# Attention scores as float32 products of 64 rows at two row positions of the array

## The chip, the cores and the metric

The kernel runs on one core of a Trainium2 chip. The metric is the time of one execution on the device in microseconds, of which the median of several runs is taken. The profile shows one execution: PE is TensorE's product, PEld its weight load (which can run behind a product), DVE is VectorE, ACT is ScalarE, POOL is GpSimd, SP is SyncE, which here issues DMAs.

## The reference

One layer of a decoder trunk on x of 512 tokens by 1024 channels (batch 1, one layer). An input projection of the normalised and modulated x gives queries, keys and values for two attentions and two gates.

```
qa, ka, va, qd, kd, vd, ga, gd = split(h @ w_in)
# sliding window: 8 query heads of 64, 2 key/value heads (4 query heads share one),
# blocks of 128 queries against the block before and their own, ALiBi, a sink per head
scores = einsum('bnqkgd,bnskd->bnkgqs', qb, kb) * 64 ** -0.5       # then mask, bias, softmax with sink, times values
# differential: 4 heads with 2 maps of 64 each, blocks of 128 queries against all keys, causal, ALiBi
scores = einsum('bqhmd,bshmd->bhmqs', qblk, k) * 64 ** -0.5
a = softmax(scores)[:, :, 0] - lam * softmax(scores)[:, :, 1]      # then times values, RMSNorm per head
merged = sigmoid(ga) * (out_a @ w_branch_swa) + sigmoid(gd) * (out_d @ w_branch_diff)
x = x + gate1 * (merged @ w_out)                                   # then a gated convolutional MLP and a last norm
```

Every score is a sum over only 64 channels. All arrays are float32.

## The kernel before

Weights and activations that go through TensorE are split into a high and a low part in the format float32r: the high part is a rounded copy (ACT), the low part is source minus high (DVE). A product of two split operands is then three TensorE instructions (`mm3`, L123 to L125: high by high, high by low, low by high). Tokens lie along the free axis: a projection unit (`steps`) multiplies eight blocks of a weight tile into one PSUM bank of 128 output channels by 512 tokens.

The stages in order of time: opening sums and modulation; the first projections over eight blocks k (`product`, into eight accumulators `acc`); the attentions with the rest of the projections; the merge; the output projection; the MLP (`up`, then `dc`).

In the attention stage TensorE's order is written out by hand (`manual_schedule`). `fill(n)` issues n steps of whatever projection unit is next (queries `pqa`, differential queries `pq` and keys `pk`, gates `pga`, branches `pA`); between the fills stand the attention's own products. The constants `SWA_FILL` and `DIFF_FILL` say how many steps lie between. ACT and DVE take their work in an order that a planner makes from priorities, `issue_after` and, at the opening of the stage, a second hand-written order.

Sliding window: four pairs i, each of the heads i and i + 4, which use the two key heads. `swa_scores(i, n0)` makes the scores of two query blocks n0 and n0 + 1 for both heads j (L581), 128 keys wide for block 0 and 256 for the others, into one bank per head (`sbank`, three in rotation). DVE adds the bias and takes the maximum (L587), ACT takes the exponential (L602), DVE normalises (L610); `swa_transpose` (L621) turns the result, and `swa_values` (L632) multiplies by the values as float32 products, the two heads at two column positions (columns 0 to 63 and 64 to 127).

Differential: 16 steps s, head h = s // 4 and query block n = s % 4, with n + 1 blocks of keys. `diff_scores` (L679) makes both maps m, 128 to 512 columns wide. Steps 0 and 1 of a head go as one group, steps 2 and 3 each alone, so there are 12 groups; the sliding window has eight.

A score's operands fill 128 rows although it sums over 64 channels. For one head, `stack` writes the query's high part (ACT) into the 64 rows that the head owns and its low part (DVE) into the other 64. `double` writes the key's high part, then its low part, into both halves of rows. Two float32r products with the same stacked query, first by the high key and then by the low key, give all four cross terms:

```
for b in range(2):
    nc.tensor.matmul(sps[j][:, n - n0, :w], qa[:, i, j, qs], ka[:, j, b, ks], start=b == 0, stop=b == 1)
```

For the first key tile and the first query tile the copies stand in the opening order by hand (L476 to L490); the low part of query pair 1 is made after the first scores. The key tile `ka` serves all four pairs; each differential head has a tile `qk` of six planes (two query planes, four key planes).

Of the kernel before, what the change touches and what calls it, by code (L numbers as in the profile page):

```python
# [8 lines left out]
F32 = mybir.dt.float32  # L9
F32R = mybir.dt.float32r  # L10
AF = mybir.ActivationFunctionType
ALU = mybir.AluOpType
PSUM = bass.MemoryType.PSUM

P = 128
D = 1024
S = 512
# [30 lines left out]
def kernel(  # L48
# [367 lines left out]

    at = ExitStack()
    ap = pool("att", stack=at)
    qa = big.tile([P, 4, 2, S], F32R, tag="qa", name="qa")
    ka = big.tile([P, 2, 2, S], F32R, tag="kvA", name="ka")  # L420
    lower, upper = slice(0, 64), slice(64, P)
    outa = [big.tile([P, 4, S], F32R, tag=f"out{g}", name=f"outa{g}") for g in "hl"]

# [6 lines left out]
            nc.vector.scalar_tensor_tensor(lo, src, scale, hi.bitcast(F32), ALU.mult, ALU.subtract)  # L430


    halves = ((lower, upper), (upper, lower))

    def stack(dst, src, scale, soon=HP, high=True, low=True):
        with tc.high_priority(offset=soon) if soon else ExitStack():
            sc = [scale if isinstance(scale, float) else scale[own] for own, _ in halves]
            for j in range(2) if high else ():
                own = halves[j][0]
                nc.scalar.activation(dst[own, j], src[own], AF.Copy, scale=sc[j])  # L440
            for j in range(2) if low else ():
                own, other = halves[j]
                nc.vector.scalar_tensor_tensor(
                    dst[other, j], src[own], sc[j], dst[own, j].bitcast(F32), ALU.mult, ALU.subtract
                )

    def double(dst, src, soon):
        with tc.high_priority(offset=soon):
            for j, (own, _) in enumerate(halves):
                nc.scalar.copy(dst[own, j, 0], src[own])  # L450
            for j, (own, _) in enumerate(halves):
                nc.vector.tensor_sub(dst[own, j, 1], src[own], dst[own, j, 0].bitcast(F32))
            for j, (own, other) in enumerate(halves):
                (nc.scalar.copy if j or soon == HP else nc.vector.tensor_copy)(dst[other, j], dst[own, j])

    vv = [big.tile([P, DIFF_HEADS, S], F32R, tag=f"vv{g}", name=f"vv{g}") for g in "hl"]
    vaT = big.tile([P, S], F32, tag="sq2", name="vaT")
# [10 lines left out]
    def load_tile(n, name):  # L468
# [4 lines left out]
    man = ExitStack()  # L473
    man.enter_context(tc.manual_schedule(engines={nc.vector.engine, nc.scalar.engine}))
    first_tiles = [load_tile(TILE_QA + i, f"wqa{i}") for i in (2, 3)]
    nc.scalar.copy(ka[lower, 0, 0], acc[0][lower])  # L476
    nc.scalar.copy(ka[upper, 1, 0], acc[0][upper])
    nc.vector.tensor_sub(ka[lower, 0, 1], acc[0][lower], ka[lower, 0, 0].bitcast(F32))
    nc.vector.tensor_sub(ka[upper, 1, 1], acc[0][upper], ka[upper, 1, 0].bitcast(F32))
    keep_v(3)  # L480
    nc.scalar.activation(qa[lower, 0, 0], acc[1][lower], AF.Copy, scale=qsc[lower, 0:1])
    nc.vector.scalar_tensor_tensor(
        qa[upper, 0, 0], acc[1][lower], qsc[lower, 0:1], qa[lower, 0, 0].bitcast(F32), ALU.mult, ALU.subtract
    )
    nc.scalar.copy(ka[upper, 0, 0], acc[0][lower])
    nc.scalar.copy(ka[upper, 0, 1], ka[lower, 0, 1])
    nc.scalar.activation(qa[upper, 0, 1], acc[1][upper], AF.Copy, scale=qsc[upper, 0:1])
    nc.vector.tensor_copy(ka[lower, 1, 0], acc[0][upper])
    nc.vector.tensor_sub(ka[lower, 1, 1], acc[0][upper], ka[lower, 1, 0].bitcast(F32))
    nc.vector.scalar_tensor_tensor(  # L490
        qa[lower, 0, 1], acc[1][upper], qsc[upper, 0:1], qa[upper, 0, 1].bitcast(F32), ALU.mult, ALU.subtract
    )
    stack(qa[:, 1], acc[2], qsc[:, 1:2], soon=0, low=False)
    keep_v(6, (0,))
    vat_copy = nc.scalar.copy(vaT, acc[5])
    man.close()
# [67 lines left out]
    def swa_scores(i, n0):  # L564
        if n0 == 0:
            c = pairs[i] = Pair()
            c.nm, c.lsum, c.es = (
                ap.tile([P, 2, NT], F32, tag=t, bufs=2, name=f"{t}{i}") for t in ("nm", "lsum", "es")
            )
            c.sb = [ap.tile([P, 2, P], F32, tag="st0", bufs=2, name=f"st{i}_0")]  # L570
            c.sb += [ap.tile([P, 2, 256], F32, tag="st", bufs=ST, name=f"st{i}_{n}") for n in range(1, NT)]
            c.pT, c.copies = [], [None, None]
        c = pairs[i]
        sps = {j: sbank(f"sw{i}_{n0}_{j}", (P, 2, 256)) for j in range(2)}
        order = [(j, n) for j in range(2) for n in (n0, n0 + 1)]
        for j, n in order if i == 0 or n0 else order[::2] + order[1::2]:
            w = P if n == 0 else 2 * P
            k0 = max(0, n - 1) * P
            qs, ks = slice(n * P, (n + 1) * P), slice(k0, k0 + w)
            for b in range(2):  # L580
                nc.tensor.matmul(sps[j][:, n - n0, :w], qa[:, i, j, qs], ka[:, j, b, ks], start=b == 0, stop=b == 1)  # L581
        for j in range(2):
            for n in (n0, n0 + 1):
                w = P if n == 0 else 2 * P
                with tc.high_priority(offset=HP):
                    h = i + 4 * j
                    c.last = nc.vector.tensor_tensor_reduce(  # L587
                        c.sb[n][:, j, :w], sps[j][:, n - n0, :w], dsw[:, 256 - w : 256], -(2.0 ** -(h + 1)),
                        nsink[:, h : h + 1], ALU.add, ALU.min, c.nm[:, j, n : n + 1],
                    )  # L590
# [50 lines left out]
    def add_q(i):  # L641
        def q(wts):
            o = fbank(f"pqa{i}")
            yield from steps(o, wts, hT, KT)
            stack(qa[:, i], o, qsc[:, i : i + 1])

        units.append((None, q))

    def add_head(h):
        def q(wts):  # L650
            t = heads[h] = ap.tile([P, 6, S], F32R, tag="qk", bufs=2, name=f"qk{h}")
            o = fbank(f"pq{h}")
            yield from steps(o, wts, hT, KT)
            stack(t[:, 0:2], o, 2.0 ** (2 * h - 1), HP if h > 1 else HP // 2)

        def k(wts):
            t = heads[h]
            o = fbank(f"pk{h}")
            yield from steps(o, wts, hT, KT)
            double(t[:, 2:6].rearrange("p (j b) s -> p j b s", b=2), o, HP if h > 1 else HP // 2)  # L660

        for run, n in ((q, TILE_QD), (k, TILE_KD)):
            units.append((lambda n=n: load_tile(n + h, f"w{n}_{h}"), run))
# [4 lines left out]
    def diff_scores(*ss):  # L668
        ops = []
        for s in ss:  # L670
            h, n = divmod(s, NT)
            t = heads[h]
            w = (n + 1) * P
            if n == 0:
                firsts[h] = [sbank(f"sd{h}_{m}", (P, 2, 256)) for m in range(2)]
            sps = [firsts[h][m][:, n, :w] if n < 2 else sbank(f"sd{h}_{n}_{m}")[:, :w] for m in range(2)]
            for m in range(2):
                for b in range(2):
                    nc.tensor.matmul(  # L679
                        sps[m], t[:, m, n * P : (n + 1) * P], t[:, 2 + 2 * m + b, :w], start=b == 0, stop=b == 1  # L680
                    )
            ops.append((s, sps, w))
        for s, sps, w in ops:
            h, n = divmod(s, NT)
            mx = ap.tile([P, 2], F32, tag="dmx", bufs=3, name=f"dmx{h}_{n}")
            pm = []
            for m in range(2):
                st = ap.tile([P, w], F32, tag="st", bufs=ST, name=f"sd{h}_{n}_{m}")
                with tc.high_priority(offset=HP):
                    nc.vector.tensor_tensor_reduce(  # L690
                        st, sps[m], ddf[:, 512 - w : 512], -(2.0 ** (-2 * (h + 1))), 3e38, ALU.add, ALU.min,
                        mx[:, m : m + 1],
                    )
                pm.append(st)
            scored[s] = mx, pm
# [149 lines left out]
    with tc.issue_after(pairs[0].last.ins), tc.issue_after(vat_copy.ins):  # L845
        with tc.high_priority(offset=HP):
            keep_v(6, (1,))
            keep_v(4, (1,))
        stack(qa[:, 1], acc[2], qsc[:, 1:2], high=False)
        swa_softmax(0)  # L850
        keep_v(7, (1,))

        lp = cpool.tile([P, 2, 64], F32, tag="part", name="lp")
        ls = cpool.tile([P, 2], F32, name="ls")
        nlam = cpool.tile([P, 1], F32, name="nlam")
        nc.vector.tensor_mul(lp, lamv[:, 0:4:2], lamv[:, 1:4:2])
        nc.vector.reduce_sum(ls, lp, axis=mybir.AxisListType.X)
        nc.scalar.activation(ls, ls, AF.Exp)
        nc.vector.tensor_sub(nlam, ls[:, 1:2], ls[:, 0:1])
        nc.vector.tensor_scalar_add(nlam, nlam, -LAM_INIT)  # L860
        fill(VA_AT)
        turn_va()
        fill(SWA_FILL[2] - VA_AT)
# [1015 lines left out]
```

## Time and profile before

| what | value |
|---|---|
| median of 3 runs | 676.56 us (676.55 to 677.2) |
| span of the profiled execution, first to last instruction | 675.4 us |
| PE busy | 665.2 us (98%), 4021 instructions |
| PEld busy | 591.5 us (88%) |
| DVE busy | 564.1 us (84%) |
| ACT busy | 400.6 us (59%) |
| POOL busy | 85.0 us (13%) |
| mean granted TensorE clock | 0.996 |
| chain that ended last | PE 84%, issue 7%, DVE 4% |

The profiled execution's own time is known only by its span; the median of the runs is 1.2 us longer, which lies around the first and the last instruction. The busy time of PE is the union of its instructions' times; products overlap in the array, their ends are modelled, and so what a product occupies is read from the distance between starts, not from its duration. A row such as "128*128 128x256" gives the loaded operand's rows and columns and then the streamed operand's rows and columns.

### The profile page before, as it was taken

What the parts mean: (1) busy time and instruction counts of PE and PEld (TensorE: products, weight loads), DVE (VectorE), ACT (ScalarE), POOL (GpSimd) and SP (SyncE); (2) the same over time, 40 slices, a digit from 0 to 9 for tenths busy, and PEclk for the clock granted to TensorE, in tenths of its full rate; (3) what the DMA queues carried; (4) which work ended last, traced back from release to release, by engine and by line L of the source; (5) the groups of instructions that cost most, each with busy time, mean ns of one, the idle gap of its engine ahead of it and who ended that gap; (6) DMA issues with size and microseconds to landing.
All of it is one profiled execution on the core that took longest, in us unless ns stands there. A gap on an engine that the chain in (4) does not pass through costs nothing.

```text
span 675.4 us, 10797 instructions
## 1 busy us (share of the span) xinstructions
PE 665.2 (98%) x4021; PEld 591.5 (88%) x4021; DVE 564.1 (84%) x1005; ACT 400.6 (59%) x704; POOL 85.0 (13%) x111
## 2 busy tenths in 40 slices
PE   8999999999999999999999999999999999999995
PEld 7888888888887888888899999999999998888884
DVE  6988997778767678954899998888888899979996
ACT  7678787465745333233696655556655666665664
POOL 2000000002213100010010211011111004441200
PEclk9999999999999999999999999999999999999998
DMA  9961231445255697568365988797886559996803
GB/s 357 417 235 62 94 95 63 132 149 179 89 170 188 236 314 264 189 185 282 92 123 137 227 201 200 203 214 162 187 198 171 132 187 208 198 203 186 157 0 125
DMA packets 72068, 121.78 MB, mean 180 GB/s; under 512 B 4240, under 2 KB 48432, under 8 KB 72016
## 3 DMA queue, kind: packets, MB, share of 16 engines
q1 hardware_dynamic: 53104, 95.04, 41.4%
q0 software_dynamic: 18624, 25.84, 22.8%
q8 instruction: 31, 0.51, 0.3%
q10 hardware_dynamic: 288, 0.21, 0.1%
q14 instruction: 21, 0.17, 0.1%
HBM read 118.97 MB, written 2.11 MB: 179 GB/s over the span
## 4 chain that ended last, share of the span: by engine, by line
PE 84%; issue 7%; DVE 4%; DMA 1%; ACT 1%; POOL 1%; POOLq 0%; ACTq 0%
PE up L1202 33%; PE dc L1808 7%; PE av L371 3%; PE oc L1262 2%; PE oc L1258 2%; PE pgd L124 2%; PE pgd L123 2%; PE oc L1259 2%; PE pgd L125 2%; PE aqa L368 2%; PE pga L123 1%; PE pga L125 1%; PE pga L124 1%; PE sw L581 1%; PE sd L679 1%
## 5 line engine op out<-in xcount | busy, mean ns | idle before, releaser
L1202 PE MATMUL up<-t,m_whi 128*128 128x256 f32 x512 | 93.1, 283 | 0.0
L1202 PEld LDWEIGHTS up<-t,m_whi 128*128 128x128 f32 x512 | 79.9, 192 | 0.0
L1202 PE MATMUL up<-t,m_wlo 128*128 128x256 f32 x256 | 72.4, 283 | 0.0
L1202 PE MATMUL up<-bh,p_whi 128*128 128x256 f32 x232 | 65.7, 283 | 0.0
L1202 PE MATMUL up<-bl,p_whi 128*128 128x256 f32 x232 | 65.7, 283 | 0.0
L1202 PE MATMUL up<-bh,p_wlo 128*128 128x256 f32 x232 | 65.7, 283 | 0.0
L1202 PEld LDWEIGHTS up<-t,m_wlo 128*128 128x128 f32 x256 | 49.2, 192 | 0.0
L1104 POOL DMA_DIRECT2D s<-in_w_up_dram x21 | 27.0, 1367 | 158.5 <-DMA s<-in_w_up_dram 104.8
L1202 PEld LDWEIGHTS up<-bh,p_whi 128*128 128x128 f32 x232 | 44.5, 192 | 0.0
L1202 PEld LDWEIGHTS up<-bl,p_whi 128*128 128x128 f32 x232 | 44.5, 192 | 0.0
L1202 PEld LDWEIGHTS up<-bh,p_wlo 128*128 128x128 f32 x232 | 44.5, 192 | 0.0
L1132 ACT CAST m_whi<-s 128x1024 fp32r<-128x1024 f32 x31 | 32.5, 1048 | 15.7 <-DVE s L1126 9.1
L795 DVE CUSTOM_DVE_ANT_0 ra<-ra,csb 128x1024 f32<-128x1024 f32 x32 | 38.6, 1219 | 3.8 <-DMA ra<-in_w_ada_t_dram 3.7
L1136 DVE TENSOR_TENSOR m_wlo<-s,m_whi 128x1024 fp32r<-128x1024 f32 x31 | 37.7, 1217 | 1.3 <-ACT m_whi L1132 1.3
L1202 PE MATMUL up<-t,p_whi 128*128 128x256 f32 x176 | 32.2, 283 | 0.0
L1202 PEld LDWEIGHTS up<-t,p_whi 128*128 128x128 f32 x176 | 27.4, 192 | 0.1
L705 ACT ACTIVATE sd<-sd,dmx 128x128 f32<-128x128 f32 (+3 forms) x32 | 17.8, 556 | 14.9 <-DVE dmx L690 14.7
L1132 ACT CAST p_whi<-wa 128x1024 fp32r<-128x1024 f32 x18 | 18.8, 1042 | 12.6 <-PE up L1202 9.0
L1209 ACT ACTIVATE gT<-a,cols 128x512 f32<-128x512 f32 x22 | 17.6, 813 | 13.4 <-DVE a L1244 13.0
L1136 DVE TENSOR_TENSOR p_wlo<-wa,p_whi 128x1024 fp32r<-128x1024 f32 x18 | 22.0, 1222 | 4.0 <-ACT p_whi L1132 2.7
L1202 PE MATMUL up<-t,p_wlo 128*128 128x256 f32 x88 | 24.9, 283 | 0.0
L1126 DVE TENSOR_TENSOR s<-s,wa 128x1024 f32<-128x1024 f32 x20 | 24.3, 1217 | 0.1
(551 smaller groups left out, 2036.4 us busy)
## 6 DMA issues: line engine op xcount, KB each, us to landing
ra<-in_w_ada_t_dram SPq DMA_DIRECT2D x32, 512.0 KB, 4.3
wa<-in_w_up_dram SPq DMA_DIRECT2D x22, 512.0 KB, 4.3
s<-in_w_up_dram SPq DMA_DIRECT2D x21, 512.0 KB, 4.7
s<-in_w_up_dram POOLq DMA_DIRECT2D x21, 512.0 KB, 6.8
adaw<-in_w_ada_t_dram SPq DMA_DIRECT2D x15, 512.0 KB, 9.9
a<-in_w_up_dram SPq DMA_DIRECT2D x11, 512.0 KB, 4.8
b<-in_w_down_dram SPq DMA_DIRECT2D x10, 512.0 KB, 4.0
w<-in_w_first_dram SPq DMA_DIRECT2D x8, 512.0 KB, 9.9
```

Of the source, the lines that this page charges most:

```text
L123: nc.tensor.matmul(o, lh, rh, start=start, stop=False)
L124: nc.tensor.matmul(o, lh, rl, start=False, stop=False)
L125: nc.tensor.matmul(o, ll, rh, start=False, stop=stop)
L371: nc.tensor.matmul(acc[i], ht[:, t : t + P], wts[k][w][:, S:], start=start, stop=stop)
L705: nc.scalar.activation(pm[m], pm[m], AF.Exp, bias=mx[:, m : m + 1], scale=-1.0, accum_out=(l0, l1)[m])
L795: nc.vector.tensor_tensor_reduce(r, r, csb, 1.0, 0.0, ALU.mult, ALU.add, late_mod[:, idx : idx + 1])
L1104: nc.gpsimd.dma_start(dst, upblock(*blk), accum_op=ALU.add)
L1126: nc.vector.tensor_add(src, src, R[J, "a11" if name == "m6" else "a12"])
L1132: nc.scalar.copy(W[J, name][0], R[J, SRC[name]])
L1136: nc.vector.tensor_sub(lo, R[J, SRC[name]], hi.bitcast(F32))
L1202: nc.tensor.matmul(o[u], w[:, k, cu], b[:, k], start=name in ("p1", "m5", "p2") and k == 0 and x == 0, stop=k == 3 and x == 2, skip_group_ ...
L1808: nc.tensor.matmul((bank2[u] if o is None else o)[:, sl], a[:, q, cu], b[:, q, sl], start=first_mm and x == 0, stop=last_mm and x == 2, sk ...
```

## The change

Queries and keys are kept as float32, once, in the 64 rows in which the projection leaves them (`keep`, one ACT instruction over all 128 rows, for the first key tile one DVE copy). The head or map j reads rows 0 to 63 or 64 to 127 (`sides[j]`) of both operands, and a score is one float32 product over 64 rows. Products of the two heads, or of the two maps, alternate, at the two row positions of the array, into two banks. `stack`, `double`, the split and the doubling are gone, and so are the hand-written copies of the opening; the tiles shrink (`qa` from eight planes to four, `ka` from four to one, `qk` from six to two). Within a group of the sliding window the order of products becomes block by block, both heads of a block together. The query of pair 1 is kept whole in the opening, where only its high part was.

```
-    qa = big.tile([P, 4, 2, S], F32R, tag="qa", name="qa")
-    ka = big.tile([P, 2, 2, S], F32R, tag="kvA", name="ka")
+    qa = big.tile([P, 4, S], F32, tag="qa", name="qa")
+    ka = big.tile([P, S], F32, tag="kvA", name="ka")
...
-    def stack(dst, src, scale, soon=HP, high=True, low=True):
...
-    def double(dst, src, soon):
...
+    sides = (lower, upper)
+
+    def keep(dst, src, scale=1.0, soon=HP):
         with tc.high_priority(offset=soon) if soon else ExitStack():
+            nc.scalar.activation(dst, src, AF.Copy, scale=scale)
...
+    nc.vector.tensor_copy(ka, acc[0])
+    keep(qa[:, 0], acc[1], qsc[:, 0:1], soon=0)
     keep_v(3)
...
-    stack(qa[:, 1], acc[2], qsc[:, 1:2], soon=0, low=False)
+    keep(qa[:, 1], acc[2], qsc[:, 1:2], soon=0)
...
-        order = [(j, n) for j in range(2) for n in (n0, n0 + 1)]
-        for j, n in order if i == 0 or n0 else order[::2] + order[1::2]:
+        order = [(j, n) for n in (n0, n0 + 1) for j in range(2)]
+        for j, n in order:
...
-            for b in range(2):
-                nc.tensor.matmul(sps[j][:, n - n0, :w], qa[:, i, j, qs], ka[:, j, b, ks], start=b == 0, stop=b == 1)
+            nc.tensor.matmul(sps[j][:, n - n0, :w], qa[sides[j], i, qs], ka[sides[j], ks], start=True, stop=True)
...
-            stack(qa[:, i], o, qsc[:, i : i + 1])
+            keep(qa[:, i], o, qsc[:, i : i + 1])
...
-            t = heads[h] = ap.tile([P, 6, S], F32R, tag="qk", bufs=2, name=f"qk{h}")
+            t = heads[h] = ap.tile([P, 2, S], F32, tag="qk", bufs=2, name=f"qk{h}")
...
-            stack(t[:, 0:2], o, 2.0 ** (2 * h - 1), HP if h > 1 else HP // 2)
+            keep(t[:, 0], o, 2.0 ** (2 * h - 1), HP if h > 1 else HP // 2)
...
-            double(t[:, 2:6].rearrange("p (j b) s -> p j b s", b=2), o, HP if h > 1 else HP // 2)
+            keep(t[:, 1], o, 1.0, HP if h > 1 else HP // 2)
...
-                for b in range(2):
-                    nc.tensor.matmul(
-                        sps[m], t[:, m, n * P : (n + 1) * P], t[:, 2 + 2 * m + b, :w], start=b == 0, stop=b == 1
-                    )
+                nc.tensor.matmul(
+                    sps[m], t[sides[m], 0, n * P : (n + 1) * P], t[sides[m], 1, :w], start=True, stop=True
+                )
...
-        stack(qa[:, 1], acc[2], qsc[:, 1:2], high=False)
```

More of the change, by code (lines that the diff above doesn't have):

```diff
@@ L430, in evac @@
             nc.vector.scalar_tensor_tensor(lo, src, scale, hi.bitcast(F32), ALU.mult, ALU.subtract)
-    halves = ((lower, upper), (upper, lower))
-    def stack(dst, src, scale, soon=HP, high=True, low=True):
+    sides = (lower, upper)
+    def keep(dst, src, scale=1.0, soon=HP):
         with tc.high_priority(offset=soon) if soon else ExitStack():
[L437 to L444, printed above, removed]
-                )
-    def double(dst, src, soon):
[L448 to L454, printed above, removed]
+            nc.scalar.activation(dst, src, AF.Copy, scale=scale)
     vv = [big.tile([P, DIFF_HEADS, S], F32R, tag=f"vv{g}", name=f"vv{g}") for g in "hl"]
@@ L475 @@
     first_tiles = [load_tile(TILE_QA + i, f"wqa{i}") for i in (2, 3)]
[L476 to L479, printed above, removed]
+    nc.vector.tensor_copy(ka, acc[0])
+    keep(qa[:, 0], acc[1], qsc[:, 0:1], soon=0)
     keep_v(3)
[L481 to L492, printed above, removed]
-    stack(qa[:, 1], acc[2], qsc[:, 1:2], soon=0, low=False)
+    keep(qa[:, 1], acc[2], qsc[:, 1:2], soon=0)
     keep_v(6, (0,))
@@ L677, in diff_scores @@
             for m in range(2):
-                for b in range(2):
-                    nc.tensor.matmul(
-                        sps[m], t[:, m, n * P : (n + 1) * P], t[:, 2 + 2 * m + b, :w], start=b == 0, stop=b == 1
-                    )
+                nc.tensor.matmul(
+                    sps[m], t[sides[m], 0, n * P : (n + 1) * P], t[sides[m], 1, :w], start=True, stop=True
+                )
             ops.append((s, sps, w))
```

## The prediction

> **What bounds the kernel now.** I read the page's first part, then PE's table of waits, then the stretch that holds the attention.
>
> ```profile
> span 675.4 us, 10797 instructions
> PE 665.2 (98%) x4021; PEld 591.5 (88%) x4021; DVE 564.1 (84%) x1005; ACT 400.6 (59%) x704; POOL 85.0 (13%) x111
> ...
> PE ava L236 <- POOL ones L131: 1.1, 1, 1.1
> PE aka L262 <- DVE cols L266: 0.5, 1, 0.5
> PE av L371 <- ACT hThA L357: 0.4, 1, 0.4
> PE od L124 <- DVE aTl L427: 0.3, 1, 0.3
> ...
> core 0: us, PE busy (x) PEld busy (x) DVE busy (x) ACT busy (x) POOL busy (x), PEclk, DMA share, GB/s
> 57.00:213.00 156.00, 155.73 (x843) 130.24 (x842) 127.09 (x344) 102.75 (x246) 17.29 (x28) 1.00 0.36 116
> ```
>
> The second fence part is complete: TensorE waits four times, 2.3 us in all, and only once, for 0.3 us, after the opening. From 57 to 213 us, where both attentions lie, it is busy 155.73 of 156 us at a granted clock of 1.00, while DVE works 127 and ACT 103 us. So a microsecond that TensorE's own queue gains or loses here is a microsecond of the kernel, and one taken from DVE or ACT is worth nothing unless TensorE was waiting for it. The later stages keep TensorE just as full, so nothing behind the attention gives a loss back. The span is 1.2 us below the median of the runs (676.56); I make the sum in the span and add the difference to the median.
>
> **What the scores cost now.** Each stretch below runs from the first score product of a group to the first product behind it; the query has all 20 stretches, and the last row is their sum.
>
> ```profile
> 59.69:60.79 1.10, 1.10 (x9) 1.00 0.00 0
> 61.49:62.53 1.04, 1.04 (x9) 1.00 0.00 0
> 67.10:68.02 0.92, 0.92 (x9) 1.00 0.00 0
> ...
> 92.49:93.51 1.02, 1.02 (x10) 1.00 0.00 0
> 97.72:98.75 1.03, 1.03 (x11) 1.00 0.00 0
> ...
> 121.78:122.48 0.70, 0.70 (x5) 1.00 0.91 332
> ...
> 201.44:202.36 0.92, 0.92 (x5) 1.00 0.00 0
> sum 18.69, PE 18.69; mean PE 0.93
> ...
> 346.44 216.11 PE up L1202 x1800
> ```
>
> The kinds are: four products of 128 columns and four of 256 (0.92 us, eight times), eight of 256 (four times), four of 384 (0.70 us, four times), four of 512 (0.92 us, four times). The up projection's 1800 products of 256 columns took 0.120 us each, so eight should take 0.96; the 1.03 at 97.72 starts on record about 0.08 before the transposes ahead have left the array, and so do four others. I take 5 x 0.08 off: 18.3 us is what the scores occupy.
>
> **What the new products cost.** No score is a float32 product now, but the sliding-window values are, two heads at two column positions (L632).
>
> ```profile
> L632 PE MATMUL oa<-pT,va x64: 272/379/431, 89.3 to 112.2; 128*64 128x256 f32 x48, 128*64 128x128 f32 x16
> ...
> 89.80 0.14 PEld L632 LDWEIGHTS oa<-pT,va 128*64 128x64 f32 x2
> ...
> 90.44 0.14 PEld L632 LDWEIGHTS oa<-pT,va 128*64 128x64 f32 x2
> ...
> 89.31:92.49 3.18, 3.18 (x32) 2.13 (x32) 0.00 (x0) 0.59 (x1) 1.00 0.45 116
> ```
>
> The source has 32 of these products (eight per pair of heads), the trace 64: a float32 product is two passes. The weight loads come two at a time, and from 89.80 to 90.44 there are three steps, so a step of 256 columns takes 0.216 us (0.64 / 3) and serves both heads at once; 128 columns take half, 0.109. (12 steps of 0.216 and 4 of 0.109 are 3.03 of the 3.18 us.) Linear in columns, 384 take 0.323 and 512 take 0.430. If two heads at two row positions overlap as these do at two column positions, a pair of score products is two steps: 0.218, 0.432, 0.646 and 0.860 us for 128 to 512 columns. The sliding window has one pair of 128 and three of 256 columns for each of four head pairs: 4 x 1.514 = 6.06. The differential one has one of each width for each of four heads: 4 x 2.156 = 8.62. Sum 14.68, against 18.3: the streaming alone gains 3.6 us.
>
> **What the two positions cost at their edges.** The same trace shows the array going into the two-position form and out of it.
>
> ```profile
> 88.77 0.39 PE L124 MATMUL pk<-hTlB,w_h 128*128 128x512 f32 x1
> 89.00 0.39 PE L125 MATMUL pk<-hThB,w_l 128*128 128x512 f32 x1
> ...
> 89.31 0.13 PEld L632 LDWEIGHTS oa<-pT,va 128*64 128x64 f32 x1 [0.35 <-issue]
> ...
> 89.58 0.36 PEld L632 LDWEIGHTS oa<-pT,va 128*64 128x64 f32 x4
> ...
> 92.17 0.14 PEld L632 LDWEIGHTS oa<-pT,va 128*64 128x64 f32 x2
> 92.49 0.30 PEld L581 LDWEIGHTS sw<-ka,qa 128*128 128x128 f32 x2 [0.17 <-DVE st L610]
> ...
> 112.13 0.14 PEld L632 LDWEIGHTS oa<-pT,va 128*64 128x64 f32 x2
> 112.44 0.30 PEld L679 LDWEIGHTS sd<-qk 128*128 128x128 f32 x2 [0.17 <-issue]
> ...
> 131.79 0.19 PEld L125 LDWEIGHTS pA<-outah,wba_l 128*128 128x128 f32 x1
> 132.02 0.19 PEld L679 LDWEIGHTS sd<-qk 128*128 128x128 f32 x1
> ...
> 149.42 0.95 PE L746 MATMUL pss<-ones,sq 128*128 128x1 f32 x8
> 150.23 0.31 PE L720 MATMUL td<-ident,sd 128*128 128x128 f32 x1
> ```
>
> Without a change of form (131.79, 132.02) the next weight load starts one product's step after the last, behind its streaming. At 89.0 it doesn't: the last full product is through at 89.00 + 0.23 = 89.23, the first loads start at 89.31, and as the second loads follow at the start of the second step, 89.58, the first step began at 89.58 - 0.216 = 89.364. Going in costs 0.084 us of emptying and 0.053 of a load of 64 columns that nothing covers. Coming out: the last step runs from 92.17 + 0.11 = 92.28 to 92.39, the next load starts at 92.49: 0.10 us of emptying, and again an uncovered load. The other exit (112.13 to 112.44) has the same 0.31 us, though the two are put down to different releasers, so I read it as the array's own. A load of 128 columns costs 0.111: the sums of one column, which only loads can bound, take 0.81 us for 7.25 steps (149.42 to 150.23). The score groups load 128 columns, so I price going in at 0.084 + 0.111 = 0.195, and out at 0.10 + 0.111 = 0.21. There are 20 groups (eight of the sliding window, twelve differential), each with ordinary projections or transposes around it. At two places (92.49, 112.44) the group follows the values directly and the emptying is paid already: there only the load, 0.111, is new, and its like today is in the 1.02 against 0.92 above. Sum: 18 x 0.195 + 2 x 0.111 + 20 x 0.21 = 7.9 us.
>
> The bounds of this price: at least nothing, if row positions switch freely; at most 0.111 more per entry, if the second head's load goes behind the first's. I take the column positions' price, the only change of form in the trace. The Trainium skill, "TensorEngine Tiling (Array Packing)", Key Properties, states that a change of the tiling mode, as against the tile alone, drains TensorE; the exits' 0.10 us agree. By that rule the sum is the one taken here; by the trace's ordinary hand-over alone it would be 3.6 us below the time before.
>
> **Copies on ACT and DVE.**
>
> ```profile
> L440 ACT ACTIVATE qa<-pqa,qsc x4: 671/683/686, 68.3 to 77.4; 64x512 fp32r<-64x512 f32 x4
> L443 DVE SCALAR_TENSOR_TENSOR qa<-pqa,qsc,qa x4: 745/750/756, 70.3 to 78.9; 64x512 fp32r<-64x512 f32 x4
> L319 DVE COPY csb<-aka x1: 685/685/685, 7.7 to 7.7; 128x512 f32<-128x512 f32 x1
> L488 DVE CAST ka<-aka x1: 693/693/693, 57.9 to 57.9; 64x512 fp32r<-64x512 f32 x1
> L440 ACT ACTIVATE qk<-pq x8: 577/593/595, 85.6 to 166.5; 64x512 fp32r<-64x512 f32 x8
> L452 DVE TENSOR_TENSOR qk<-pk,qk x8: 678/689/697, 96.4 to 176.5; 64x512 fp32r<-64x512 f32 x8
> L454 ACT CAST qk<-qk x6: 1047/1049/1051, 99.2 to 177.6; 64x1024 fp32r<-64x1024 f32 x6
> ```
>
> A copy over all 128 rows takes what one of 64 rows takes (0.685 for csb, 0.693 for ka, both from a bank of 512 columns). ACT loses four of eight query copies (2.7 us), four key copies at about the 0.59 of the row of pq (2.3), eight of sixteen differential ones at the same price (4.7) and six doublings (6.3): 16 us. DVE loses eight subtractions of 0.75, three of four key operations of 0.69, sixteen of 0.69 and two doublings of 0.69: 20.5 us. I cost this at zero: TensorE's stream of projections covers all of it, since in this stage it waits 0.3 us in all. What it can give is that 0.3, and the uneven first two groups (1.10 against 0.92, 1.04 against 0.96, about 0.26 us), which wait for halves of ka and qa; the latter is in the sum already, as I replace the whole 18.3. The copy of head pair 1 moves ahead of the first scores, one ACT operation of 0.68 in the place of two, so what is queued behind it comes sooner. No added operation waits for anything new, no DMA is issued or moved, and no SP or POOL queue is passed. The scores of n now come for both heads before the next n, so DVE's first read may wait one pair longer (0.43 us); nothing on TensorE waits for that read within three banks.
>
> **The sum.** 14.68 + 7.9 - 18.3 = +4.3 us: 676.56 + 4.3 = 680.9.
>
> **The rivals.**
>
> *Row positions need no emptying.* The price of the edges falls to nothing and the kernel ends at 676.56 - 3.6 = 672.9. It decides once a round trip costs under 3.6 / 20 = 0.18 us instead of 0.40. For it: no row of the trace shows row positions. Against it: both column entries and exits pay. The half-way case, round trips of 0.11 to 0.25 us, ends within 0.2% (1.35 us, about what this kernel's runs can tell from no change).
>
> *The two heads' weight loads go one after the other.* A pair of 128 columns then needs four loads, 0.444 in the place of 0.218 (8 x 0.226 = 1.8), one of 256 columns 0.444 for 0.432 (16 x 0.012 = 0.2), and each entry shows a second load (20 x 0.111 = 2.2): 4.3 + 4.2 = 8.5, 685.1 us. Against it: the 64-column loads start two at a time; for it: those are different columns, these the same columns in different rows.
>
> *No overlap of the two row positions.* The streaming doubles: 4.3 + 14.7 = 19.0, 695.6 us. Against it stand the doubled steps of L632. The Trainium skill, "TensorE: Matmul & The Clock Gate", Part 3, reports 3.07 times the rate for four row tiles, which speaks for overlap; no run here shows it yet.
>
> **How the numbers follow.** The forecast 0.52, its own range 679.3 to 682.5; loads in turn 0.14; no overlap 0.12; free switching 0.11; the half-way case 0.11. So faster by over 0.2% 0.11, within 0.2% 0.11, slower 0.78. The range 673.0 to 687.0 goes from free switching to loads in turn with 2 us beside it, and leaves out the case without overlap.
>
> **What will show it.** The score lines should have 128 passes as now (64 products, two passes each), of 64 rows, starting two at a time, with steps of 0.11, 0.22, 0.32 and 0.43 us; weight loads in pairs; before and behind each group a gap on the weight loads of 0.2 us or so; the 20 stretches with their edges near 22.6 us; PE's waits still under 0.5 us in the stage; DVE's and ACT's busy time 20 and 16 us lower; every later stage the same length, later by about 4 us. I am wrong if loads follow each other without that gap, if the two heads' passes start a whole pass apart, or if freed ACT and DVE time shortens a stage in which TensorE stands full.

## The result and the profile after

The changed kernel takes 681.45 us (median of four runs, 681.21 to 682.81) against 676.57: a ratio of 1.0074 with a 95% interval of 1.0061 to 1.0086, 4.9 us more. The forecast was 680.9.

The page's first rows of the changed kernel, then PE's whole table of waits, then the attention's stretch:

```profile
span 679.2 us, 10744 instructions
PE 669.8 (99%) x4021; PEld 583.7 (86%) x4021; DVE 545.3 (80%) x976; ACT 384.8 (57%) x682; POOL 85.4 (13%) x111
```

```profile
PE ava L236 <- POOL ones L131: 1.1, 1, 1.1
PE av L371 <- ACT hThA L357: 0.4, 1, 0.4
```

```profile
57.00:213.00 156.00, 156.00 (x823) 118.60 (x822) 104.44 (x312) 87.69 (x226) 17.04 (x28) 1.00 0.35 109
```

DVE is 19 us less busy and ACT 16, TensorE 4.6 us more: the freed engines stand idle beside a TensorE that has no idle time on record left in the stage. These savings are those of the whole execution; the same window holds less of a stage that grew, so its 22.7 us less of DVE overstate them. The stretches of the scores, from the first product of a group to the first product behind it (the same query as before, 20 stretches):

```profile
59.76:60.62 0.86, 0.86 (x9) 1.00 0.00 0
61.51:62.69 1.18, 1.18 (x9) 1.00 0.00 0
67.46:68.31 0.86, 0.86 (x9) 1.00 0.00 0
72.82:73.89 1.06, 1.06 (x9) 1.00 0.97 354
...
123.13:123.97 0.85, 0.85 (x5) 1.00 0.56 111
...
205.77:206.83 1.06, 1.06 (x5) 1.00 0.68 186
sum 18.84, PE 18.84; mean PE 0.94
```

The sum looks like that of before (18.69), because half of the edges lies outside the stretches. The next rows, PE and PEld around one differential group of 384 columns, show the edges:

```profile
122.57 0.39 PE L124 MATMUL pA<-outal,wba_h 128*128 128x512 f32 x1
122.80 0.40 PE L125 MATMUL pA<-outah,wba_l 128*128 128x512 f32 x1
123.13 0.92 PE L646 MATMUL sd<-qk 64*128 64x384 f32 x4
123.97 0.50 PE L123 MATMUL pga<-hThA,wga_h 128*128 128x512 f32 x1
124.31 0.40 PE L124 MATMUL pga<-hTlA,wga_h 128*128 128x512 f32 x1
```

```profile
122.58 0.19 PEld L125 LDWEIGHTS pA<-outah,wba_l 128*128 128x128 f32 x1
123.12 0.30 PEld L646 LDWEIGHTS sd<-qk 64*128 64x128 f32 x4 [0.36 <-issue]
...
123.97 0.19 PEld L123 LDWEIGHTS pga<-hThA,wga_h 128*128 128x128 f32 x1 [0.54 <-issue]
```

The product at 122.80 is through at 123.03, the first score load starts at 123.12: 0.09 us of emptying. Behind the group the first full product is recorded at 123.97, the second only at 124.31: 0.34 where 0.23 is the rule, so 0.11 of an uncovered load. Within the stretch lie the entry's load (0.11), two steps of 0.32 and the exit's emptying (0.10): 0.85. With 18 x 0.09 for the entries that were not paid before and 20 x 0.11 behind the groups, the scores occupy 18.84 + 3.8 = 22.6 us, the figure that the prediction gave. One group stands out: the second takes 1.18 us where the others of its kind take 1.06, as there alone the second head's first load starts 0.12 us behind the first head's; what holds it is not shown.

How much the stage lost is read between two products that frame it: the last one of the first projections, and behind the last group the low-part product of the fourth gate's last block. Their rows in the kernel before, in a second trace of that kernel (below), and in the changed one:

```profile
58.10 0.39 PE L371 MATMUL av<-whi,hTlB 128*128 128x512 f32 x1
...
202.59 0.39 PE L124 MATMUL pga<-hTlB,wga_h 128*128 128x512 f32 x1
```

```profile
57.88 0.39 PE L371 MATMUL av<-whi,hTlB 128*128 128x512 f32 x1
...
202.35 0.39 PE L124 MATMUL pga<-hTlB,wga_h 128*128 128x512 f32 x1
```

```profile
58.08 0.39 PE L371 MATMUL av<-whi,hTlB 128*128 128x512 f32 x1
...
207.17 0.40 PE L124 MATMUL pga<-hTlB,wga_h 128*128 128x512 f32 x1
```

They lie 144.49 us apart in the first trace of before, 144.47 in the second and 149.09 in the changed kernel: the stage lost 4.60 us. The score lines themselves, from the views of the tiles `sw` and `sd`, have the same 128 passes as before, now of 64 rows and with the longer durations of float32:

```profile
L549 PE MATMUL sw<-ka,qa x64: 272/376/481, 59.8 to 99.6; 64*128 64x256 f32 x48, 64*128 64x128 f32 x16
...
L646 PE MATMUL sd<-qk x64: 272/430/694, 113.7 to 206.3; 64*128 64x128 f32 x16, 64*128 64x256 f32 x16, 64*128 64x384 f32 x16, 64*128 64x512 f32 x16
```

### The profile page after: what moved, and what is told of

The parts are those of the page before. It is cut to its first block, busy times and chain, and to the rows that moved or that the text cites. A ratio compares the mean times of both kernels' runs of the same rounds, so it can differ in the third digit from the quotient of the medians.

```text
span 679.2 us, 10744 instructions
## 1 busy us (share of the span) xinstructions
PE 669.8 (99%) x4021; PEld 583.7 (86%) x4021; DVE 545.3 (80%) x976; ACT 384.8 (57%) x682; POOL 85.4 (13%) x111
## 3 DMA queue, kind: packets, MB, share of 16 engines
q0 software_dynamic: 18624, 25.84, 22.6%
HBM read 118.97 MB, written 2.11 MB: 178 GB/s over the span
## 4 chain that ended last, share of the span: by engine, by line
PE 90%; issue 7%; DVE 2%; POOL 1%; ACT 0%; POOLq 0%
PE up L1168 33%; PE dc L1774 7%; PE av L371 3%; PE pga L123 2%; PE pga L125 2%; PE pga L124 2%; PE oc L1224 2%; PE pgd L123 2%; PE oc L1228 2%; PE pgd L124 2%; PE oc L1225 2%; PE pgd L125 2%; PE sd L646 2%; PE aqa L368 2%; PE pk L123 1%
## 5 line engine op out<-in xcount | busy, mean ns | idle before, releaser
L1098 ACT CAST p_whi<-wa 128x1024 fp32r<-128x1024 f32 x18 | 18.8, 1045 | 12.6 <-PE up L1168 10.8
```

Source lines behind the costliest of these rows:

```text
L1098: nc.scalar.copy(W[J, name][0], R[J, SRC[name]])
```

## The experiments

### One attention at a time

```
e1: qa, ka and swa_scores as changed; stack, double, the six-plane qk and the old diff_scores kept
e2: qk, keep and diff_scores as changed; the old qa, ka and swa_scores kept
```

> Only the sliding window's eight groups become float32 products of 64 rows; the differential scores stay split and doubled. If each change of the array's form costs about 0.2 us and the streaming gains, as the forecast has it: four groups of 128 and 256 columns lose 0.65 + 0.405 - 0.92 = 0.13 us each, four of 256 columns 0.86 + 0.405 - 0.96 = 0.31 each, less 0.2 where the entry behind the values was paid already and 0.26 of the uneven first groups: the span grows by about 1.3 us. If the loss came from copies or order and not from the groups, it would not divide by groups: anything between 0 and 4.

> Only the twelve differential groups change. By the price of the edges: four of 0.65 + 0.405 - 0.92 = 0.13 us (one with its entry paid), eight of 0.65 or 0.86 + 0.405 - 0.70 or 0.92 = 0.35: about 3.2 us in the stage, less up to 0.6 if the two late waits of TensorE near 207 and 211 us go as in the changed kernel: span +2.6 to +3.2, and with the first experiment the sum gives the span of the changed kernel (+3.8). If the two parts share a cause, the two spans add to less.

The sliding window alone: 678.56 us, ratio 1.0034 (1.0022 to 1.0046), span 676.1. The differential scores alone: 680.61 us (679.82 to 681.66), 1.0057 (1.0045 to 1.0070), span of the profiled execution 677.8. The kernel before had spans of 674.4 to 675.3 in the runs beside these, with 674.6 the commonest. By the medians of the runs the parts cost 2.0 and 4.0 us, more than both at once (4.9), so the times alone do not show that the parts add up. The traces do: the two products that frame the stage, with the sliding window alone and then with the differential scores alone:

```profile
58.01 0.39 PE L371 MATMUL av<-whi,hTlB 128*128 128x512 f32 x1
...
203.80 0.39 PE L124 MATMUL pga<-hTlB,wga_h 128*128 128x512 f32 x1
```

```profile
57.94 0.39 PE L371 MATMUL av<-whi,hTlB 128*128 128x512 f32 x1
...
205.72 0.40 PE L124 MATMUL pga<-hTlB,wga_h 128*128 128x512 f32 x1
```

They lie 145.79 and 147.78 us apart, against 144.49 before: 1.30 and 3.29, together 4.59, where both at once cost 4.60. The loss divides by groups as priced (1.3 and 3.2).

### More changes of form, the same products

```
 in swa_scores, behind the first block's pair; in diff_scores, between steps 0 and 1 of a head:
+                fill(1)
 the fill behind the group:
-        fill(SWA_FILL[3])
+        fill(SWA_FILL[3] - more)
 (and likewise SWA_FILL[1], VA_AT, SWA_FILL[5], DIFF_FILL[0], DIFF_FILL[2])
```

> The changed kernel, with one projection step (three full products) moved from behind each of the twelve two-block groups into its middle. Products, operands and copies are the same; the array changes its form twelve times more in each direction. If a round trip costs 0.405 us, as the forecast has it, the span grows by 4.9 us over the changed kernel (684.1). If the loss comes from the float32 passes or anything else in the groups and not from their edges, the span stays within 0.5 us of 679.2.

686.67 us, ratio 1.0148 (1.0131 to 1.0165), span 684.4: 5.2 over the changed kernel. Two products that both kernels have, one ahead of and one behind ten of the split groups, first in the changed kernel, then in this one, and last the one wait of PE that only this one has:

```profile
66.90 0.40 PE L124 MATMUL pqa<-hTlA,wqa_h 128*128 128x512 f32 x1
...
188.20 0.39 PE L124 MATMUL pA<-outal,wba_h 128*128 128x512 f32 x1
```

```profile
68.38 0.39 PE L124 MATMUL pqa<-hTlA,wqa_h 128*128 128x512 f32 x1
...
193.70 0.40 PE L124 MATMUL pA<-outal,wba_h 128*128 128x512 f32 x1
```

```profile
PE sw L549 <- DVE nm L557: 0.5, 1, 0.5
```

The lag grows from 1.48 to 5.50 us over ten splits: 0.402 us for a round trip, with nothing but the order of products changed. That is the price of the forecast (0.405). The first two groups don't count: moving their step left none between them, so they ran into one another, and TensorE waited 0.5 us for a bank there.

### Float32 without row positions

```
-    qa = big.tile([P, 4, S], F32, tag="qa", name="qa")
+    qa = big.tile([P, 4, 2, S], F32, tag="qa", name="qa")    # each head's query in its own rows, zeros in the other 64
-            nc.tensor.matmul(sps[j][:, n - n0, :w], qa[sides[j], i, qs], ka[sides[j], ks], start=True, stop=True)
+            nc.tensor.matmul(sps[j][:, n - n0, :w], qa[:, i, j, qs], ka[:, ks], start=True, stop=True)
 (diff_scores alike; GpSimd writes the zeros)
```

> Scores as float32 products over all 128 rows: each head's query in its own 64 rows and zeros in the other 64, keys as in the changed kernel. No row positions, so no change of form, but no overlap of heads either. By the forecast's terms the streaming is 2 x 14.68 = 29.4 us against 18.3 and the edges cost nothing: span +11 us over the kernel before (686.5), without a gap on the weight loads at the groups' edges. If going between float32r and float32 itself empties the array, the gaps stay and the span is +17 to +19 (693).

687.81 us, ratio 1.0163 (1.0148 to 1.0178), span 686.0: 11.4 over the usual 674.6 of before, where 11 was expected. PEld and PE around the same first group of head pair 1:

```profile
67.44 0.19 PEld L125 LDWEIGHTS pqa<-hThA,wqa_l 128*128 128x128 f32 x1
67.67 0.53 PEld L561 LDWEIGHTS sw<-ka,qa 128*128 128x128 f32 x3
```

```profile
67.44 0.40 PE L124 MATMUL pqa<-hTlA,wqa_h 128*128 128x512 f32 x1
67.67 0.40 PE L125 MATMUL pqa<-hThA,wqa_l 128*128 128x512 f32 x1
67.91 1.47 PE L561 MATMUL sw<-ka,qa 128*128 128x128 f32 x8
69.03 0.58 PE L123 MATMUL pqa<-hThA,wqa_h 128*128 128x512 f32 x1
```

The first load of the float32 scores starts with the last float32r product (67.67 both), no gap stands on the row, and the group is at work 0.24 us after that product's start. So going in from float32r to float32 costs nothing; the gap belongs to the row positions. For the way out no row is shown, but 11.4 us against 11 leaves no room for 20 edges of 0.2. Without row positions each head streams by itself, and the loss is larger: the overlap is worth more than the edges cost.

### The heads in turn

```
-        order = [(j, n) for n in (n0, n0 + 1) for j in range(2)]
+        order = [(j, n) for j in range(2) for n in (n0, n0 + 1)]
```

> The changed kernel with the sliding window's products in the order of the heads: both blocks of head 0, then both of head 1. If only neighbours in the queue overlap, a group of four 256-column products takes seven steps of 0.216 us instead of four (+0.65 each, four groups) and one of 128 and 256 columns about +0.45 (four groups): span +4 to +5 us over the changed kernel (683.5). If the array takes products of the free row position ahead of their turn, the span stays at 679.2.

682.18 us (681.30 to 682.40), ratio 1.0077 (1.0062 to 1.0092), span of the profiled execution 679.2: as the changed kernel. Its rows around the second group, between the products that frame the stage:

```profile
58.02 0.39 PE L371 MATMUL av<-whi,hTlB 128*128 128x512 f32 x1
...
61.13 0.40 PE L125 MATMUL pqa<-hThA,wqa_l 128*128 128x512 f32 x1
61.46 1.24 PE L549 MATMUL sw<-ka,qa 64*128 64x256 f32 x8
62.63 0.50 PE L123 MATMUL pqa<-hThA,wqa_h 128*128 128x512 f32 x1
...
207.15 0.40 PE L124 MATMUL pga<-hTlB,wga_h 128*128 128x512 f32 x1
```

The group lasts 1.17 us as it does with alternating heads (1.18), though both products of head 0 stand ahead of head 1's in the source, and the whole stage takes 149.13 us against 149.09. The views list starts and not the order in which TensorE gets its products; that it is the source's is borne out by the semaphores in the packed trace, where the last product of each of these eight groups adds more than one to its count here, and one in the changed kernel. So each row position takes its own next pass, and the alternation that the change writes out is not what makes the heads overlap. My expectation of 4 to 5 us was wrong. The Trainium skill, "TensorE: Matmul & The Clock Gate", Part 3, has products strictly in program order in start and end; here, where two row positions are free, the measured length of the group says otherwise.

### What lies outside the span

The changed kernel's runs are 2.04 to 2.11 us longer than their spans, and the table ahead of the prediction made that 1.2 for the kernel before. I took the difference for a real 0.9 us, and a code load behind the end of the program for its cause.

```
     keep_warm(10)
+    pad = cpool.tile([P, 1], F32, name="pad")
+    for _ in range(40):                        # 8 in the control
+        nc.vector.memset(pad, 0.0)
```

> The changed kernel with 40 one-column memsets on DVE in its idle opening. The time outside the span grew from 1.15 to 2.06 us with the change; in its trace a code load of 8 KB falls 1.7 us behind the program's last instruction, where the kernel before had its last such load 5 us ahead of the end, when DVE had done 1218 instructions; the change takes 38 instructions from DVE. If that load is what lies outside, 40 more bring it back into the span: time less span 1.1 to 1.2 us, total about 0.9 us under the changed kernel (680.5), span unchanged. If the time outside comes from something else, it stays at 2.0 to 2.1 and the total at 681.4.

> The same with 8 memsets, as a control: DVE ends 30 instructions short of the kernel before, so by the code load the time outside stays 2.0 to 2.1 us and the total near 681.4. If any padding or shift of addresses moves it, it falls here too.

Both theories of these texts fall. With 40 memsets the runs are 2.04 to 2.11 us longer than their spans (682.27 us, span of the profiled execution 679.3), with 8 they are 2.03 to 2.11 (681.38 us, span 679.3); the padding does nothing. What lies outside the span differs from kernel to kernel (2.3 to 2.5 us with the sliding window alone, 1.7 to 1.8 with full rows), and no run shows why. And the ten runs of the kernel before beside them are 1.88 to 1.95 us longer than their own spans. There never were 0.9 us, only 0.15: the profiled execution of before was one of its longer ones, and its time was not 676.56.

### A second trace of the kernel before

> The kernel before, unchanged, for a second trace. Its runs beside the experiments have spans of 674.4 to 675.3 us, mostly 674.6, with 1.9 us outside; the profiled execution of before has 675.4. If that one was held up by a late load of a gate's weights (5.5 us, in its chain ahead of the waits near 207 and 211 us), a second trace has a span of 674.6, no wait of TensorE behind the opening, and the product that stood at 202.6 us is no later while those behind 211 us come 0.6 us sooner. If the waits belong to the kernel, they are there again and the changed kernel removed them.

676.31 us, span 674.4. PE's waits in it, then its rows at the end of the attention, then the same rows of the first trace:

```profile
PE ava L236 <- POOL ones L131: 1.1, 1, 1.1
PE av L371 <- ACT hThA L357: 0.4, 1, 0.4
```

```profile
209.94 0.40 PE L123 MATMUL od<-aTh,vvh 128*128 128x512 f32 x1
210.17 0.47 PE L124 MATMUL od<-aTl,vvh 128*128 128x512 f32 x1
```

```profile
210.34 0.40 PE L123 MATMUL od<-aTh,vvh 128*128 128x512 f32 x1
210.99 0.50 PE L124 MATMUL od<-aTl,vvh 128*128 128x512 f32 x1 [0.25 <-DVE aTl L427]
```

The first trace stood 0.65 us between the two products, the second 0.23. Between the product at 202.35 or 202.59 and this one the second trace gains 0.58 us; the 0.24 ahead of them arose in the opening (0.22 at 58.10). So the wait that I had counted among those of the kernel belongs to one execution of it. What caused it is not settled: the first trace's chain goes through a gate's weights that took 5.5 us to land there, while the slowest in the second took 4.9.

### Three float32r terms at the row positions

```
+    TERMS = ((0, 0), (0, 1), (1, 0))              # high by high, high by low, low by high
-            nc.tensor.matmul(sps[j][:, n - n0, :w], qa[sides[j], i, qs], ka[sides[j], ks], start=True, stop=True)
+            nc.tensor.matmul(
+                sps[j][:, n - n0, :w], qa[sides[j], i, a, qs], ka[sides[j], b, ks], start=z == 0, stop=z == 2
+            )
 (keep writes a high part on ACT and a low part on DVE; diff_scores alike)
```

> Row positions as in the changed kernel, but queries and keys split into float32r parts in their own 64 rows, and three products (high by high, high by low, low by high) in the place of one of float32; the fourth, smallest term is left out. If the two positions overlap for any type and the edges cost 0.405 us per group, the streaming falls from 14.68 to 12.5 us (three steps of 0.111 us for 128 and 256 columns, where the loads bound, 0.163 for 384 and 0.216 for 512) and the span is 2.2 us under the changed kernel: 677.0, still 2.4 over the kernel before. If float32r passes do not overlap at row positions, it is about 689; if the edges were due to float32, it falls under 674.6 - 5 = 669.

679.77 us, ratio 1.0051 (1.0034 to 1.0068), span of the profiled execution 677.9: 1.3 under the changed kernel instead of 2.2, and still 3.3 over the usual span of before. The two positions do overlap for float32r, and the edges stay, so float32 is not their cause. The way into a differential group, from PE and from PEld:

```profile
122.46 0.40 PE L125 MATMUL pA<-outah,wba_l 128*128 128x512 f32 x1
```

```profile
122.79 0.47 PEld L654 LDWEIGHTS sd<-qk 64*128 64x128 f32 x6 [0.36 <-issue]
```

The full product is through at 122.69, and the first score load starts 0.10 us later, as with float32. PE's rows for the group that stands at 72.82 in the changed kernel are, in this one:

```profile
72.86 0.98 PE L554 MATMUL sw<-ka,qa 64*128 64x256 f32 x12
73.77 0.50 PE L123 MATMUL pqa<-hThA,wqa_h 128*128 128x512 f32 x1
74.10 0.40 PE L124 MATMUL pqa<-hTlA,wqa_h 128*128 128x512 f32 x1
```

Behind it the second full product follows the first by 0.33 us where 0.23 is the rule: the uncovered load is there too. This stretch is 0.91 us (72.86 to 73.77) against 1.06, 0.15 less where two pairs of 0.333 for 0.432 should give 0.20. All 20 stretches sum to 17.29 us against 18.84, 1.55 less where 2.2 was expected. So of the missing 0.9 us some 0.65 lies in the stretches and 0.1 in the opening; why the stretches are longer than expected is open.

## Why the prediction was right

*The bound.* TensorE's stream decides the stage, and freed ACT and DVE time is worth nothing there: confirmed by 156.00 busy us of 156 with 18.8 us less of DVE work in the execution (20.5 was added up, but no time hung on it).

*The streaming.* Two heads at two row positions overlap as two column positions do. The 128 passes are 64 rows tall, the steps are 0.32 us for 384 columns as extrapolated, and at the entry shown above four loads fit into 0.30 us, where one alone takes 0.19: they start in twos. The step of 0.216 us is printed as 0.64 / 3, which gives 0.213; the starts in the trace stand 0.216 apart, so the sum holds. That rules out the rivals of loads in turn and of no overlap.

*The edges.* The price taken from an entry and two exits of the values, with a load of 128 columns, was 0.405 us a round trip; ten added round trips cost 0.402 each. The load's 0.111 rested on 7.25 steps that no row counts; behind each group it shows itself, 0.34 less 0.23. That rules out free switching, the rival on the other side, and the half-way case. What the Trainium skill calls a drain on a change of the tiling mode ("TensorEngine Tiling (Array Packing)", Key Properties) is thus shown here for row positions too: 0.09 us of emptying going in, 0.10 coming out. The full-row experiment and the three float32r terms show that the type is not what empties the array.

*The sum.* The scores' new occupancy was forecast as 14.68 + 7.9 = 22.6 and is 22.6. The old one, 18.3, holds by its rows: 18.69 less five starts on record 0.08 early. Yet the stage lost 4.60 us and not 4.3 (4.64 with the heads in turn). The sum lacked a term: by the starts in the traces, the 416 products of 512 columns in the stage that do not stand next to a score group take 0.25 us more together than before (0.24 with the heads in turn and 0.16 with full rows, while the two traces of before differ by 0.01). That is 0.6 ns each, which no single row shows, and its cause stays open.

*The base.* "The span is 1.2 us below the median; I add the difference" was wrong: the profiled execution was not a median one. The runs of before lie 1.84 to 1.95 us over their spans, and its usual span is 674.6. As I added a difference to the median and not a span, the error left the forecast alone; it misled me only afterwards. Of the 0.55 us between 680.9 and 681.45, 0.3 is what the stage lost beyond the sum, and 0.15 that the changed kernel's runs lie further over their spans (2.04 to 2.11), which no run explains.

*Waits.* The 0.3 us of wait near 211 us that the change could have given was not the kernel's to give.

No version here beats the kernel before. A group gains 0.27 us of streaming at best (one pair of 128 and one of 256 columns) and pays 0.40. Only three groups come out ahead, by some 0.05 us each: the two that directly follow the values (1.02 before, 0.86 and an uncovered load of 0.11 now), as their way in is paid already, and the uneven first one (1.10 before, 0.86 and edges of 0.20 now). That is under what a run can tell.

## What to carry to other kernels

Price a change of the array's form by itself: where products at row or column positions stand in short groups between full products, every group pays two empty passages and two uncovered loads, here 0.40 us, so a group must save more than that in streaming. Look for a place in the trace where the same kind of change already happens, and measure from the last full product to the first load, and from the first load to the second step. And take the difference of two kernels between the same two products in both traces, or from executions of the same kind: one profiled execution stood 0.8 us off the kernel's usual span.

## What the runs showed that I had not expected

Two row positions work off their passes apart from each other: with both products of head 0 ahead of both of head 1 the group takes 1.17 us, as with alternating heads. Ordinary products between the groups took 0.25 us more in sum, though nothing about them had changed. And one wait of 0.25 us, in a stage that is otherwise full, was not there in the next trace of the same kernel.
